# Moving the first V weights' low halves from GpSimd to VectorE, with newly searched order tables, in a one-core kernel of a hybrid attention and RWKV-7 layer

## The chip, the cores and the metric

The kernel runs on one core of one Trainium2 chip. The metric is the device time of one execution in microseconds (us); lower is better. The engines are TensorE (PE in the profile, with PEld for its weight loads), VectorE (DVE), ScalarE (ACT), GpSimd (POOL) and SyncE (SP), which issues nearly all DMA transfers here. Each engine carries out its own queue of instructions in the order in which the program wrote them.

## The reference

One layer of a decoder trunk, with sequence length 512 and width 1024, in float32:

```
ada = c @ w_ada + b_ada                       # 6 x 1024: shift, scale, gate for two blocks
h = rms_norm(x, norm1_w) * (1 + sc1) + sh1
proj = h @ w_in                               # attention q/k/v, RWKV-7 r/k/v and low rank, gates
y_att = attention_mixer(att_in) @ w_att_out   # three groups (window, dilation), combined by softmax
y_rwkv = rwkv7_mixer(rwkv_in, ...) @ w_rwkv_out
x = x + gt1 * ((g_att * y_att + g_rwkv * y_rwkv) @ w_o)
h = rms_norm(x, norm2_w) * (1 + sc2) + sh2
x = x + gt2 * conv_ffn(h, w_up, conv_w, conv_b, w_down)
return rms_norm(x, norm_f_w)
```

The RWKV mixer first mixes each of its inputs with that of the token before: z + (z_prev - z) * mu. That is the "shift" of the kernel.

## The kernel before, in words

**Split products.** Each large product is made of three matmuls. A matrix a is split into a high half, a cast to a shorter format, and a low half, the difference `a - hi`. The product is then hi*hi + hi*lo + lo*hi (`gemm`, and the same by single matmuls in `body`). For weights, ScalarE casts the high half and VectorE subtracts to get the low one (`split_w`, `weights`: `whi` and `wlo`, L1397 and L1400; 128x1024 numbers at a time). For the hidden state h the names are `hhi` and `hlo`.

**Order of the work.** Nothing runs in the order in which it is written up to about 740 us. The functions `start`, `attention` and `rwkv` hand tasks to the class `Plan`: an engine, an estimated time, the function that emits the instructions, the tasks that it depends on, a priority, and the buffers that it takes and gives back. `Plan.run` (from L245) then plays a small simulation of the engines. Whenever an engine is free, it takes the ready task of the lowest priority number for which buffers are free, and emits its instructions. So the queues of all five engines, SP's DMA queue among them, come out of this simulation. Two tables correct it. `RANKS` adds a number to the priority of a kind of task (the key is engine, name, function and base priority). `HOLDS` gives the time for which TensorE must have run large matmuls before it turns to a task with small ones (its names are in `FEW`). From about 740 us on (RWKV's output product, the mixing with `w_o`, and the convolutional feed-forward) the order is that of the code.

**The start (0 to about 58 us).** The program loads x, runs some matmuls without use to warm TensorE up, and makes the shift `sh` and the scale `g1c` of the first adaptive norm in four chunks of 256 columns. For one chunk, eight blocks `araw` of w_ada, 256 KB each, come by DMA through SP's queue; VectorE multiplies and adds them up into `acc` (L708 for the first block, L710 for the others); TensorE sums over the partitions (`ada`); VectorE adds biases (`biased`, L734 to L736). Meanwhile TensorE transposes x (`tr`, `turn`); ScalarE scales (`ht`, L750) and casts (`hhi`, L757), and VectorE makes `hlo` (L754). With each part of h that is done, two products begin: `early` (the first q and k columns: `rows`, L767, high half L774, low half L777) and `v` (the first V columns, 256 of them: `v_load` L781, `v_hi` on ScalarE L787, `v_lo` on GpSimd L790). The V weights come in four loads `wvraw` of 128x2x256 numbers each, with two buffers.

**The middle (58 to about 740 us).** Products (`body`) with names such as `qk`, `v`, `lg`, `r`, `k` run on TensorE, between them the small matmuls of attention and RWKV. Two PSUM buffers ("mm") hold the results of these products. An RWKV product's buffer is given back when `shift` has read it: ScalarE writes a scaled, moved copy to `sh`, then VectorE adds the rest (L1410). Around 310 us, at the end of attention, VectorE scales the heads' outputs `o` by their shares `pw` (L1283, from PSUM), GpSimd adds the groups into `attT` (L1287), and the RWKV part's low-rank input `lg` and first `r` product are under way; `lg` is shifted into `lt` and its low half is made by L1424 (`la`, `lw`). The sums `xy`, `inv` and their like later are the steps of RWKV's chunked inverse.

Of the kernel before, what the change touches and what calls it, by code (L numbers as in the profile page):

```python
# [39 lines left out]
class Task:  # L40
# [19 lines left out]
    ('ACT', 'gate hi', 'hi', 69.0): -15.59,  # L60
    ('ACT', 'gate hi', 'hi', 70.0): -48.82,
    ('ACT', 'gate hi', 'hi', 79.0): 145.29,
    ('ACT', 'pack', '<lambda>', 3.0): 141.26,
    ('ACT', 'pe', '<lambda>', 0.5): -6.53,
    ('ACT', 'qk01', 'out', 1.0): 75.76,
    ('ACT', 'qk02 hi', 'hi', 16.0): 90.45,
    ('ACT', 'qk11 hi', 'hi', 26.0): 171.77,
    ('ACT', 'r0 hi', 'hi', 41.0): -15.37,
    ('ACT', 'shift', '<lambda>', 1.0): -48.66,
    ('ACT', 'v', 'out', 1.0): 223.26,  # L70
    ('ACT', 'v0 hi', 'hi', 42.0): -7.9,
    ('ACT', 'v12 hi', 'hi', 32.0): -40.94,
    ('ACT', 'v4 hi', 'hi', 54.0): 94.86,
    ('ACT', 'v6 hi', 'hi', 60.0): 83.03,
    ('ACT', 'v7 hi', 'hi', 63.0): 247.01,
    ('DMA', '', 'g2_load', 2.0): 45.89,
    ('DMA', 'ada', 'load', 2.0): 0.01,
    ('DMA', 'ada', 'load', 4.0): 0.08,
    ('DMA', 'ada', 'load', 13.0): -168.52,
    ('DMA', 'ada', 'load', 15.0): -44.69,  # L80
    ('DMA', 'ada', 'load', 21.0): 4.66,
    ('DMA', 'ada', 'load', 26.0): -4.53,
    ('DMA', 'ada', 'load', 34.0): 1.61,
    ('DMA', 'ada', 'load', 44.0): 15.07,
    ('DMA', 'ada', 'load', 46.0): 17.01,
    ('DMA', 'gate', 'load', 64.0): 9.03,
    ('DMA', 'gate', 'load', 66.0): -6.21,
    ('DMA', 'gate', 'load', 67.0): -17.61,
    ('DMA', 'gate', 'load', 73.0): 127.85,
    ('DMA', 'gate', 'load', 76.0): 3.06,  # L90
    ('DMA', 'gate', 'load', 79.0): 177.78,
    ('DMA', 'lg', 'load', 38.0): -6.6,
    ('DMA', 'pa', 'load', 81.0): -34.81,
    ('DMA', 'pa', 'load', 84.0): -56.19,
    ('DMA', 'pa', 'load', 85.0): -6.11,
    ('DMA', 'pa', 'load', 86.0): -82.28,
    ('DMA', 'pa', 'load', 87.0): -28.22,
    ('DMA', 'pr', 'load', 88.0): 3.83,
    ('DMA', 'pr', 'load', 89.0): 1.56,
    ('DMA', 'qk11', 'load', 26.0): -1.88,  # L100
    ('DMA', 'qk12', 'load', 18.0): -4.01,
    ('DMA', 'qk12', 'load', 30.0): -4.2,
    ('DMA', 'r0', 'load', 41.0): -3.39,
    ('DMA', 'r4', 'load', 53.0): -23.25,
    ('DMA', 'v rows', 'v_load', 2.5): 0.85,
    ('DMA', 'v rows', 'v_load', 3.5): -0.05,
    ('DMA', 'v rows', 'v_load', 5.5): -0.77,
    ('DMA', 'vec', 'load', 2.0): 0.01,
    ('DMA', 'vec', 'load', 10.0): -33.87,
    ('DVE', '', '<lambda>', 200.0): -147.45,  # L110
    ('DVE', '', '<lambda>', 200.2): -44.67,
    ('DVE', '', '<lambda>', 200.3): 4.02,
    ('DVE', '', '<lambda>', 200.4): -161.3,
    ('DVE', '', '<lambda>', 200.6): -199.61,
    ('DVE', '', '<lambda>', 220.0): -140.0,
    ('DVE', '', 'diagonal', 200.25): -181.98,
    ('DVE', '', 'diagonal', 200.65): -127.76,
    ('DVE', '', 'gated', 150.0): -114.98,
    ('DVE', '', 'k_row', 200.0): -171.17,
    ('DVE', '', 'k_row', 200.2): -185.79,  # L120
    ('DVE', '', 'k_row', 200.6): 0.74,
    ('DVE', '', 'l2_lo', 1.0): -18.87,
    ('DVE', '', 'r_k', 200.2): -200.85,
    ('DVE', '', 'scaled', 200.65): -190.19,
    ('DVE', '', 'var', 150.0): 253.2,
    ('DVE', 'ada', 'step', 1.5): 239.91,
    ('DVE', 'ada', 'step', 46.0): -43.16,
    ('DVE', 'gate lo', 'lo', 68.0): 335.19,
    ('DVE', 'pts', 'turned', 1.02): 8.9,
    ('DVE', 'qk10 lo', 'lo', 6.0): 29.84,  # L130
    ('DVE', 'qk11 lo', 'lo', 13.0): 93.21,
    ('DVE', 'scan', '<lambda>', 200.7): -137.91,
    ('DVE', 'shift', '<lambda>', 1.0): 110.56,
    ('DVE', 'v1 lo', 'lo', 45.0): 21.1,
    ('DVE', 'v12 lo', 'lo', 19.0): 36.25,
    ('DVE', 'vec', '<lambda>', 1.0): -1.64,
    ('PE', 'ada', 'cols', 1.0): 47.99,
    ('PE', 'ada', 'rows', 1.0): 9.01,
    ('PE', 'early', '<lambda>', 10.21): 35.75,
    ('PE', 'early', '<lambda>', 10.5): 18.33,  # L140
    ('PE', 'early', '<lambda>', 10.6): 1.32,
    ('PE', 'gate', '<lambda>', 73.0): -81.73,
    ('PE', 'gate', '<lambda>', 75.0): -73.35,
# [2536 lines left out]
```

## Time and profile before

| | |
|---|---|
| median of 3 runs | 1179.42 us (1178.59 to 1179.48) |
| the profiled execution's own time | 1178.59 us |
| its span in the profile | 1176.9 us |
| share of the span busy | PE 98%, PEld 80%, DVE 63%, ACT 46%, POOL 12% |
| instructions on DVE and POOL | 1245 and 275 |
| moved by DMA | 138.94 MB |

The profile is that of one execution. A row of a timeline gives the start in us from the span's beginning, the duration, engine, line, operation, output and inputs by the program's names with their shapes, how many alike were put together, and in brackets the idle time of the engine before it with what ended it. A row of the stretches gives the busy us of PE, PEld, DVE, ACT and POOL with instruction counts, TensorE's granted clock (1.00 is full speed), the busy share of the DMA engines and their GB/s. A row of the waits gives who waited for whom, the total in us, how often, and the longest. All matmuls go through the helper at L339 and all transposes through L342, so one tells them apart by their outputs' names.

### The profile page before, as it was taken

How to read it: one execution, taken by the hardware profiler on the slowest of the kernel's cores; microseconds unless marked ns; L12 is line 12 of the kernel's file. 1: busy time of each engine (PE TensorE's matmuls, PEld its weight loads, DVE VectorE, ACT ScalarE, POOL GpSimd, SP SyncE). 2: the span in 40 equal slices, each digit the busy share in tenths (PEclk: the TensorE clock that was granted, in tenths of full speed). 3: DMA queues.
4: the chain of work that ended last, by engine and by line, in shares of the span. 5: the costliest groups of instructions: out<-in, count | busy, mean ns of one | idle time of the engine just before them, and what ended most of it. 6: DMA issues, size and time to landing. Idle time of an engine off the chain costs nothing.

```text
span 1176.9 us, 19259 instructions
## 1 busy us (share of the span) xinstructions
PE 1158.0 (98%) x7552; PEld 939.6 (80%) x7552; DVE 744.4 (63%) x1245; ACT 541.8 (46%) x1012; POOL 137.5 (12%) x275
## 2 busy tenths in 40 slices
PE   8999999999999999999999999999999999999997
PEld 8888888798677777778877777888888888888886
DVE  6688857423778988656897665844666565552236
ACT  5466524424466374565635653534444444432123
POOL 6110000000300022340101441023000000000001
PEclk9999999999999999999999999999999999999999
DMA  9756767120332332322241526631333333333231
GB/s 326 230 159 187 215 187 220 52 68 19 96 94 73 104 106 75 104 85 87 80 115 59 191 69 197 206 116 37 90 90 101 96 92 106 90 114 101 90 126 72
DMA packets 168330, 138.94 MB, mean 118 GB/s; under 512 B 8785, under 2 KB 150315, under 8 KB 168239
## 3 DMA queue, kind: packets, MB, share of 16 engines
q1 hardware_dynamic: 168095, 137.39, 38.4%
q8 instruction: 59, 0.97, 0.4%
q10 hardware_dynamic: 144, 0.33, 0.1%
q14 instruction: 32, 0.26, 0.1%
HBM read 127.39 MB, written 10.30 MB: 117 GB/s over the span
## 4 chain that ended last, share of the span: by engine, by line
PE 87%; DVE 7%; DMA 3%; ACT 1%; issue 1%; SPq 1%; POOL 0%; POOLq 0%; DVEq 0%; ACTq 0%
PE u L339 23%; PE o L339 13%; PE qk L339 9%; PE v L339 8%; PE pg L339 8%; PE pr L339 4%; PE k L339 3%; PE r L339 3%; PE pa L339 2%; PE pt L342 2%; PE xy L339 2%; PE sc L339 2%; DMA araw<-in_w_ada_dram 1%; PE xo L339 1%; PE po L339 1%
## 5 line engine op out<-in xcount | busy, mean ns | idle before, releaser
L385 DVE TENSOR_TENSOR wlo<-raw,whi 128x1024 fp32r<-128x1024 f32 x65 | 79.6, 1224 | 133.8 <-ACT whi L384 133.8
L339 PE MATMUL u<-h2hi,whi 128*128 128x512 f32 (+2 forms) x368 | 140.6, 382 | 0.0
L339 PE MATMUL u<-h2lo,whi 128*128 128x512 f32 (+2 forms) x368 | 140.6, 382 | 0.0
L339 PE MATMUL u<-h2hi,wlo 128*128 128x512 f32 (+2 forms) x368 | 140.5, 382 | 0.0
L1397 ACT CAST whi<-raw 128x1024 fp32r<-128x1024 f32 (+1 forms) x73 | 72.5, 993 | 122.0 <-PE qk L339 51.1
L384 ACT CAST whi<-raw 128x1024 fp32r<-128x1024 f32 x65 | 68.5, 1054 | 91.6 <-PE o L339 53.7
L1400 DVE TENSOR_TENSOR wlo<-raw,whi 128x1024 fp32r<-128x1024 f32 (+1 forms) x73 | 86.5, 1184 | 31.2 <-ACT whi L1397 31.0
L339 PEld LDWEIGHTS u<-h2lo,whi 128*128 128x128 f32 x368 | 69.1, 188 | 13.4 <-POOL h2lo L596 0.2
L339 PEld LDWEIGHTS u<-h2hi,whi 128*128 128x128 f32 x368 | 69.1, 188 | 13.2
L339 PEld LDWEIGHTS u<-h2hi,wlo 128*128 128x128 f32 x368 | 69.1, 188 | 12.9
L2495 DVE SCALAR_TENSOR_TENSOR u<-u,cols,u 128x511 f32<-128x511 f32 x88 | 65.7, 746 | 4.3 <-ACT u L2493 2.7
L339 PE MATMUL qk<-hhi,whi 128*128 128x512 f32 x160 | 63.4, 396 | 0.0
L339 PE MATMUL qk<-hhi,wlo 128*128 128x512 f32 x160 | 63.1, 394 | 0.0
L339 PE MATMUL qk<-hlo,whi 128*128 128x512 f32 x160 | 62.8, 393 | 0.0
L339 PE MATMUL o<-whi,fhi 128*128 128x512 f32 x144 | 56.1, 390 | 0.3 <-DVE u L2495 0.3
L339 PE MATMUL o<-wlo,fhi 128*128 128x512 f32 x144 | 56.0, 389 | 0.0
L339 PE MATMUL o<-whi,flo 128*128 128x512 f32 x144 | 56.0, 389 | 0.0
L339 PE MATMUL pg<-hhi,whi 128*128 128x512 f32 x128 | 52.2, 408 | 0.4 <-DVE v L1410 0.4
L339 PE MATMUL pg<-hhi,wlo 128*128 128x512 f32 x128 | 51.8, 405 | 0.0
L339 PE MATMUL pg<-hlo,whi 128*128 128x512 f32 x128 | 51.6, 403 | 0.0
L538 DVE SCALAR_TENSOR_TENSOR acc<-araw,cols,acc 128x1024 f32<-128x1024 f32 x28 | 35.8, 1279 | 19.3 <-DMA araw<-in_w_ada_dram 19.1
L1043 DVE CUSTOM_DVE_ANT_0 sm<-sc,m 128x256 f32<-128x256 f32 (+1 forms) x64 | 23.8, 402 | 32.0 <-PE sc L339 30.8
(462 smaller groups left out, 2778.7 us busy)
## 6 DMA issues: line engine op xcount, KB each, us to landing
raw<-in_w_in_dram SPq DMA_DIRECT2D x62, 512.0 KB
raw<-in_w_up_dram SPq DMA_DIRECT2D x44, 512.0 KB
araw<-in_w_ada_dram SPq DMA_DIRECT2D x32, 512.0 KB
raw<-in_w_down_dram SPq DMA_DIRECT2D x22, 512.0 KB
araw<-in_w_ada_dram SPq DMA_DIRECT2D x32, 256.0 KB
wvraw<-in_w_in_dram SPq DMA_DIRECT2D x20, 256.0 KB
raw<-in_w_rwkv_out_dram SPq DMA_DIRECT2D x8, 512.0 KB
raw<-in_w_o_dram SPq DMA_DIRECT2D x8, 512.0 KB
```

The costliest lines, as they stand in the source:

```text
L339: return self.nc.tensor.matmul(out, lhsT, rhs, start=start, stop=stop)
L342: self.nc.tensor.matmul(out, in_, self.ident[: in_.shape[0], : in_.shape[0]], is_transpose=True, start=start, stop=stop,)
L384: self.nc.scalar.copy(hl[0], raw)
L385: (lo_eng or self.nc.vector).tensor_tensor(hl[1], raw, hl[0], op=ALU.subtract)
L538: nc.vector.scalar_tensor_tensor(d["acc"], raw, ck, d["acc"], op0=ALU.mult, op1=ALU.add)
L1043: nc.vector.tensor_tensor_reduce(d["sm", h][:, :wd], d["sc"][h][:, :wd], m[:, 256 - wd : 256] if gi == 0 else m[:, :wd], 1.0, 3.0e38, op0= ...
L1397: nc.scalar.copy(d["w"][0], d["raw"])
L1400: nc.vector.tensor_tensor(d["w"][1], d["raw"], d["w"][0], op=ALU.subtract)
L2495: nc.vector.scalar_tensor_tensor(u[:, d:], pu[:, : S - d], ch(c), u[:, d:], op0=ALU.mult, op1=ALU.add)
```

## The change

There are two edits. In `start`, the function `v_lo` subtracts on VectorE in place of GpSimd, and its task is given to VectorE's queue with an estimate of 0.7 us in place of 1.6. And the tables `RANKS` and `HOLDS` are replaced by others: nearly all entries differ, and so the simulation gives all queues another order up to about 740 us. The program is 7 lines shorter, so a line of the kernel after has a number lower by 7 (L1410 is L1403 after).

```diff
 RANKS = {
-    ('DMA', 'v rows', 'v_load', 2.5): 0.85,
-    ('DVE', 'shift', '<lambda>', 1.0): 110.56,
...
             def v_lo(c=c, w=w):
-                nc.gpsimd.tensor_tensor(vd["w"][1][:, 2 * c : 2 * c + 2], w["v"], vd["w"][0][:, 2 * c : 2 * c + 2],
+                nc.vector.tensor_tensor(vd["w"][1][:, 2 * c : 2 * c + 2], w["v"], vd["w"][0][:, 2 * c : 2 * c + 2],
                                         op=ALU.subtract)
...
-            vt = pool(1.6, v_lo, [t], 2.1, give=("wvraw",), name="v lo")
+            vt = dve(0.7, v_lo, [t], 2.1, give=("wvraw",), name="v lo")
```

GpSimd has 261 instructions in its queue in place of 265, VectorE 1238 in place of 1234, TensorE 5007 rows in both, of the same matmuls. Runs of matmuls of 256 or more columns are broken by smaller ones 199 times in place of 202. Three places follow, of the two programs apart.

SyncE's DMA queue at the start, between the w_ada blocks of chunk 2 and those of chunk 3 (`araw`); `wvraw` are V weights, `raw` with x2 the q and k weights of `early`, `raw` of 128x8x128 a weight load of `body`. Before:

```order
L781 DMA wvraw_364<-in_w_in_dram 128x2x256
L781 DMA wvraw_371<-in_w_in_dram 128x2x256
L767 DMA raw_378<-in_w_in_dram 128x2x256 x2
L369 DMA raw_394<-in_w_in_dram 128x8x128
L700 DMA araw_409<-in_w_ada_dram 128x2x256
```

The same place after:

```order
L774 DMA wvraw_364<-in_w_in_dram 128x2x256
L760 DMA raw_371<-in_w_in_dram 128x2x256 x2
L362 DMA raw_384<-in_w_in_dram 128x8x128
L362 DMA raw_401<-in_w_in_dram 128x8x128
L774 DMA wvraw_415<-in_w_in_dram 128x2x256
L693 DMA araw_423<-in_w_ada_dram 128x2x256
```

A second `body` load has moved ahead of chunk 3's blocks, and the second V load behind the q, k and `body` loads.

VectorE's queue at the end of chunk 3 and the beginning of chunk 4 (`acc` are the sums of w_ada blocks, `wv` the V weights' halves, `sh` and `g1c` the biases' results). Before:

```order
L710 SCALAR_TENSOR_TENSOR acc_453<-araw_471,cols,acc_453 128x512
L710 SCALAR_TENSOR_TENSOR acc_453<-araw_481,cols,acc_453 128x512
L708 TENSOR_SCALAR acc_549<-araw_518,cols 128x512
L710 SCALAR_TENSOR_TENSOR acc_549<-araw_527,cols,acc_549 128x512
L734 TENSOR_TENSOR sh_111<-ada_551,cols 128x2
L735 TENSOR_TENSOR g1c<-ada_551,cols 128x2
L736 SCALAR_TENSOR_TENSOR g1c<-g1c,cols 128x2
L710 SCALAR_TENSOR_TENSOR acc_549<-araw_533,cols,acc_549 128x512
```

The same place after:

```order
L703 SCALAR_TENSOR_TENSOR acc_469<-araw_488,cols,acc_469 128x512
L703 SCALAR_TENSOR_TENSOR acc_469<-araw_495,cols,acc_469 128x512
L783 TENSOR_TENSOR wv_392<-wvraw_415,wv_391 128x512
L701 TENSOR_SCALAR acc_548<-araw_521,cols 128x512
L727 TENSOR_TENSOR sh_111<-ada_536,cols 128x2
L728 TENSOR_TENSOR g1c<-ada_536,cols 128x2
L729 SCALAR_TENSOR_TENSOR g1c<-g1c,cols 128x2
L770 TENSOR_TENSOR wlo_542<-raw_501,whi_541 128x1024
L703 SCALAR_TENSOR_TENSOR acc_548<-araw_527,cols,acc_548 128x512
```

One of the four moved subtractions stands behind chunk 3's last block, and the biases stand one block earlier in chunk 4.

VectorE's queue around 310 us of the profile before (`o` scaled by `pw`, then the low halves and the shifts; `lt<-lg` is the shift of the low-rank input). Before:

```order
L1283 TENSOR_TENSOR o_117<-o_117,pw_3049 128x512
L1283 TENSOR_TENSOR o_117<-o_117,pw_3054 128x512
L1283 TENSOR_TENSOR o_117<-o_117,pw_3059 128x512
L1283 TENSOR_TENSOR o_117<-o_117,pw_3069 128x512
L1400 TENSOR_TENSOR wlo_3066<-raw_2984,whi_3065 128x1024
L1424 TENSOR_TENSOR la<-lt_2993,la 64x512
L1410 SCALAR_TENSOR_TENSOR lt_3095<-lg_3001,mu_2_121,sh 32x512
L1400 TENSOR_TENSOR wlo_3098<-raw_2853,whi_3097 128x1024
L1410 SCALAR_TENSOR_TENSOR k_3119<-r_2979,mu_120,sh 128x512
```

The same place after:

```order
L1263 TENSOR_TENSOR share<-pe_3038,share 8x512
L1403 SCALAR_TENSOR_TENSOR lt_3058<-lg_2989,mu_2_121,sh 32x512
L1276 TENSOR_TENSOR o_117<-o_117,pw_3061 128x512
L1393 TENSOR_TENSOR wlo_3055<-raw_2977,whi_3054 128x1024
L1276 TENSOR_TENSOR o_117<-o_117,pw_3063 128x512
L1276 TENSOR_TENSOR o_117<-o_117,pw_3072 128x512
L1276 TENSOR_TENSOR o_117<-o_117,pw_3087 128x512
L1428 TENSOR_SCALAR lt_3058<-lt_3058 32x512
L1393 TENSOR_TENSOR wlo_3100<-raw_1901,whi_3099 128x1024
L1403 SCALAR_TENSOR_TENSOR k_3122<-k_2961,mu_120,sh 128x512
```

The shift of `lg` has moved ahead of the four scalings and of the low half `wlo`, and the split `la` no longer stands here but about thirty rows earlier.

More of the change, by code (lines that the diff above doesn't have):

```diff
@@ L60 @@
[L60 to L95, printed above, removed]
@@ L108 @@
[L108 to L131, printed above, removed]
@@ new lines @@
+    ('ACT', 'pts', 'turned', 1.0): 211.5,
+    ('ACT', 'qk01', 'out', 1.0): 29.09,
+    ('ACT', 'qk01 hi', 'hi', 12.0): 49.1,
+    ('ACT', 'qk12 hi', 'hi', 17.0): -28.85,
+    ('ACT', 'r4 hi', 'hi', 53.0): -52.65,
+    ('ACT', 'v0 hi', 'hi', 42.0): 167.12,
+    ('ACT', 'v12 hi', 'hi', 19.0): 218.37,
+    ('ACT', 'v4 hi', 'hi', 54.0): 202.52,
+    ('DMA', 'ada', 'load', 2.0): -35.02,
+    ('DMA', 'ada', 'load', 3.0): -14.22,
+    ('DMA', 'ada', 'load', 19.0): 1.45,
+    ('DMA', 'ada', 'load', 25.0): -1.05,
@@ new lines @@
+    ('DMA', 'ada', 'load', 35.0): -1.19,
+    ('DMA', 'gate', 'load', 64.0): 1.55,
+    ('DMA', 'gate', 'load', 67.0): -2.21,
+    ('DMA', 'gate', 'load', 68.0): 6.69,
+    ('DMA', 'gate', 'load', 69.0): -6.31,
+    ('DMA', 'gate', 'load', 73.0): 116.59,
+    ('DMA', 'gate', 'load', 79.0): 160.33,
+    ('DMA', 'lg', 'load', 38.0): -12.76,
+    ('DMA', 'lg', 'load', 39.0): 1.1,
+    ('DMA', 'pa', 'load', 81.0): 4.99,
+    ('DMA', 'qk00', 'load', 4.0): -4.27,
+    ('DMA', 'qk00', 'load', 5.0): -4.9,
@@ new lines @@
+    ('DMA', 'qk01', 'load', 11.0): -5.78,
+    ('DMA', 'qk01', 'load', 25.0): -5.77,
+    ('DMA', 'qk02', 'load', 29.0): 5.91,
+    ('DMA', 'qk11', 'load', 27.0): 6.78,
+    ('DMA', 'r7', 'load', 62.0): -1.38,
+    ('DMA', 'rows', 'rows', 2.5): -19.57,
+    ('DMA', 'rows', 'rows', 3.5): -7.21,
+    ('DMA', 'v rows', 'v_load', 2.5): -6.43,
+    ('DMA', 'v1', 'load', 45.0): -21.04,
+    ('DMA', 'v2', 'load', 48.0): 13.86,
+    ('DMA', 'v4', 'load', 54.0): -22.65,
+    ('DMA', 'vec', 'load', 2.0): -50.64,
@@ new lines @@
+    ('DMA', 'x', 'load', 2.0): -53.8,
+    ('DVE', '', '<lambda>', 0.0): -46.28,
+    ('DVE', '', '<lambda>', 1.0): -46.33,
+    ('DVE', '', '<lambda>', 200.0): -5.42,
+    ('DVE', '', '<lambda>', 200.1): -222.9,
+    ('DVE', '', '<lambda>', 200.2): -264.85,
+    ('DVE', '', '<lambda>', 200.3): 114.14,
+    ('DVE', '', 'g2_lo', 150.0): -138.65,
+    ('DVE', '', 'k_row', 200.2): -147.35,
+    ('DVE', '', 'l2_lo', 1.0): 200.47,
+    ('DVE', '', 'r_k', 200.6): -190.77,
+    ('DVE', '', 'recip', 200.25): -179.41,
```

211 lines of the change are left out of this document (109 added, 102 removed).

## The prediction

> **What bounds the kernel now.** I read the page first, then the table of stretches, then the chain's waits on TensorE, then the timelines of TensorE, VectorE, GpSimd and ScalarE around the waits. From the page:
>
> ```profile
> span 1176.9 us, 19259 instructions
> PE 1158.0 (98%) x7552; PEld 939.6 (80%) x7552; DVE 744.4 (63%) x1245; ACT 541.8 (46%) x1012; POOL 137.5 (12%) x275
> ```
>
> TensorE is busy for 1158.0 of 1176.9 us. The change leaves its matmuls as they are and only reorders them, so the whole prize is 18.9 us of idle time plus what a lowered clock adds. GpSimd, with 137.5 us, is not a bound anywhere by its own time. The stretches (busy us of PE, PEld, DVE, ACT and POOL with their instruction counts, then the granted clock, the DMA share and GB/s) tell where to look:
>
> ```profile
> 20.00:40.00 20.00, 17.65 (x106) 15.09 (x106) 18.58 (x25) 7.82 (x11) 9.17 (x10) 1.00 1.10 342
> 300.00:320.00 20.00, 17.43 (x75) 11.87 (x74) 17.56 (x27) 8.65 (x16) 6.63 (x5) 0.92 0.30 93
> 360.00:420.00 60.00, 58.62 (x417) 46.79 (x418) 53.60 (x97) 29.21 (x45) 2.59 (x7) 1.00 0.31 87
> 580.00:620.00 40.00, 39.67 (x313) 31.88 (x313) 37.63 (x74) 15.87 (x23) 1.22 (x5) 1.00 0.37 103
> 23.35:26.76 3.41, 1.96 (x9) 1.30 (x7) 3.30 (x4) 1.70 (x3) 2.07 (x2) 1.00 1.15 319
> 37.00:40.42 3.42, 2.21 (x16) 1.67 (x14) 2.97 (x3) 0.62 (x1) 3.01 (x2) 1.00 1.09 348
> 40.42:43.83 3.41, 2.98 (x12) 2.86 (x13) 3.31 (x9) 2.69 (x4) 0.00 (x0) 0.50 1.15 322
> 313.48:316.90 3.42, 1.02 (x5) 0.52 (x3) 3.36 (x3) 1.04 (x1) 2.74 (x2) 1.00 0.47 145
> 316.90:320.31 3.41, 3.24 (x8) 2.56 (x9) 2.80 (x4) 1.77 (x3) 0.79 (x2) 0.50 0.57 179
> ```
>
> In the two 20-us stretches TensorE is idle for 2.35 and 2.57 us while VectorE is nearly full. Inside each lies a piece of 3.41 us at clock 0.50. Each such piece follows one in which TensorE was little busy (2.21 and 1.02 of 3.42 us). Work that took 2.98 us at half clock would take 1.49 at full clock, so the pieces cost 1.5 and 1.6 us. TensorE's waits, in us in total, times and longest:
>
> ```profile
> PE v L339 <- DVE lt L1410: 2.6, 1, 2.6
> PE ada L339 <- DVE acc L710: 1.8, 2, 1.6
> PE tr L342 <- DVE g1c L735: 1.4, 1, 1.4
> PE k L339 <- DVE k L1410: 0.9, 1, 0.9
> PE pg L339 <- DVE v L1410: 0.4, 1, 0.4
> ```
>
> The three waits above 1 us are all for VectorE, and all lie in those two stretches. These are where the change can give, and the terms of the sum.
>
> **The move from GpSimd to VectorE (20 to 58 us).** Timelines (start, us, engine, line, operation, idle time before and what ended it) of GpSimd, VectorE, ScalarE and TensorE:
>
> ```profile
> 24.69 3.24 POOL L790 TENSOR_TENSOR wv<-wvraw,wv 128x512 fp32r<-128x512 f32 x2 [1.77 <-ACT wv L787]
> 37.00 3.02 POOL L790 TENSOR_TENSOR wv<-wvraw,wv 128x512 fp32r<-128x512 f32 x2 [9.06 <-ACT wv L787]
> 25.17 1.64 DVE L710 SCALAR_TENSOR_TENSOR acc<-araw,cols,acc 128x512 f32<-128x512 f32 x1
> 29.66 1.22 DVE L1400 TENSOR_TENSOR wlo<-raw,whi 128x1024 fp32r<-128x1024 f32 x1
> 30.84 0.69 DVE L754 TENSOR_TENSOR hlo<-ht,hhi 128x512 fp32r<-128x512 f32 x1
> 31.45 0.74 DVE L710 SCALAR_TENSOR_TENSOR acc<-araw,cols,acc 128x512 f32<-128x512 f32 x1
> 38.91 1.65 DVE L710 SCALAR_TENSOR_TENSOR acc<-araw,cols,acc 128x512 f32<-128x512 f32 x1
> 40.56 0.14 DVE L735 TENSOR_TENSOR g1c<-ada,cols 128x2 f32<-128x2 f32 x1
> 28.12 1.05 ACT L1397 CAST whi<-raw 128x1024 fp32r<-128x1024 f32 x1 [0.77 <-DMA raw<-in_w_in_dram]
> araw<-in_w_ada_dram SPq DMA_DIRECT2D x32, 256.0 KB
> 26.86 1.05 PE L339 MATMUL ada<-few,acc 128*128 128x1 f32 x8 [1.55 <-DVE acc L710]
> 37.62 1.02 PE L339 MATMUL ada<-few,acc 128*128 128x1 f32 x8 [0.26 <-DVE acc L710]
> 40.85 1.09 PE L342 MATMUL tr<-ident,xt 128*128 128x128 f32 x4 [1.38 <-DVE g1c L735]
> ```
>
> The four L790 subtractions take about 1.6 us each on GpSimd (3.24 / 2, 3.02 / 2). While one runs, a VectorE instruction with two SBUF inputs is stretched: the same accumulation L710 takes 1.64 and 1.65 us beside GpSimd and 0.74 without it, a loss of 0.9 us each time. So the change removes at least two such losses, 1.8 us of VectorE. It adds four subtractions of 128x512 to VectorE. The trace does not show them there; the equal shape L754 takes 0.69, which I take, 4 x 0.69 = 2.8 us. The lower bound is 0.62 (half of the 1.22 that L1400 takes for twice the columns), the upper 1.6 (if something else on GpSimd runs beside it). VectorE's total thus hardly changes (+1.0 us); what changes is when each step ends.
>
> Walk of chunk 2 of adaLN: the accumulation that starts at 25.17 ends at 25.9 in place of 26.8, so TensorE's *ada* sums start at 26.0 and 0.85 of the 1.55 us wait goes. Then the new subtraction (to 26.6) and wlo (to 27.9) stand ahead of the biases and g1c (to 28.2 with three at 0.14); TensorE has its v product meanwhile, so this costs nothing unless v's own weights come late. A second body weight load is now queued on SP ahead of chunk 3's first araw. ScalarE's cast shows that a body weight landed at about 28.1; three transfers of 256 KB at 342 GB/s take 2.3 us, so that araw lands near 30.4, and VectorE waits there for about 0.9 us. Eight accumulations then end chunk 3 at 37.5, where it ended before; the 0.26 us wait becomes about 0.85. Chunk 4's first step and the biases follow one subtraction and are not stretched: g1c ends at about 39.5 instead of 40.7. TensorE has its sums and 12 v matmuls until 39.9, so the 1.38 us wait at the transpose goes. In all 1.8 + 1.4 = 3.2 us of waits become 1.8: **1.4 us gained**. If the piece from 37.00 is then busy enough, the half clock after it goes too: **1.5 us**. Term: -2.9; bounds +0.5 (the waits at chunk 3 become longer and the half clock stays) to -4.2 (all the waits but 0.5 go).
>
> **The order at 300 to 320 us.** VectorE, GpSimd and TensorE:
>
> ```profile
> 311.96 2.35 DVE L1400 TENSOR_TENSOR wlo<-raw,whi 128x1024 fp32r<-128x1024 f32 x1
> 314.34 1.90 DVE L1424 TENSOR_TENSOR la<-lt,la 64x512 fp32r<-64x512 f32 x1
> 316.28 0.74 DVE L1410 SCALAR_TENSOR_TENSOR lt<-lg,mu,sh 32x512 f32<-32x512 f32 x1
> 310.12 3.10 POOL L1287 TENSOR_TENSOR attT<-o,o 128x512 f32<-128x512 f32 x2 [11.77 <-DVE o L1283]
> 314.16 3.47 POOL L1287 TENSOR_TENSOR attT<-o,o 128x512 f32<-128x512 f32 x2 [0.94 <-DMA att_d<-attT]
> 317.07 0.79 PE L339 MATMUL v<-hhi,whi 128*128 128x512 f32 x1 [2.57 <-DVE lt L1410]
> ```
>
> TensorE has no PSUM buffer for v until the shift L1410 has read lg. The shift itself takes 0.74 us; it stands behind a wlo of 2.35 (1.22 alone) and an la of 1.90, both stretched by GpSimd's attT. In the new order the shift stands right behind *share*, ahead of four o scalings and of wlo; la was done far earlier. So 2.57 us of wait and 1.6 us of half clock go. The new order has three shorter exposures instead: lg's own buffer behind *share* (one 0.7 us instruction), the last o scaling pw_3087 behind wlo (it waits about 0.75 us), and v's next buffer (0.35): 1.8 us. Term: 2.57 + 1.6 - 1.8 = **-2.4**, with bounds 0 (the last scaling and the k shift, now behind a stretched wlo, hold TensorE as long as lt did) and -4.2 (none of the three is exposed).
>
> **The rest of the order.** Counted in the two orders, a run of matmuls of 256 columns or more is broken by small ones 202 times before and 199 after. A break costs about 0.2 us:
>
> ```profile
> 280.47 0.72 PE L339 MATMUL sc<-qk,qk 64*128 64x128 f32 x8
> 281.12 0.50 PE L339 MATMUL lg<-hhi,wlo 128*128 128x512 f32 x1
> 281.45 0.40 PE L339 MATMUL lg<-hhi,whi 128*128 128x512 f32 x1
> ```
>
> After the small sc matmuls 0.33 us pass from the start of the first large one to that of the next. Undisturbed, such a step is half of the 0.43 that it takes at half clock, 0.22 us:
>
> ```profile
> 318.09 0.63 PE L339 MATMUL v<-hhi,wlo 128*128 128x512 f32 x1
> 318.52 0.63 PE L339 MATMUL v<-hhi,whi 128*128 128x512 f32 x1
> ```
>
> So leaving a break costs 0.11 us; I choose the same for entering one, 0.2 in all. Term: 3 x 0.2 = **-0.6**, bounds 0 and -0.6. Everything from about 740 us on stands in the same order and is taken at nothing. Elsewhere (60 to 300, 320 to 740 us) the new tables reorder much, but the largest of TensorE's waits there are the 0.9 and 0.4 us above, so little is to be had and more can be lost: see the rivals.
>
> **Sum.** -2.9 - 2.4 - 0.6 = -5.9 against the profiled execution's 1178.59 us (its span 1176.9 and 1.69 around it): 1172.7. That execution was 0.83 us below the median of the three runs, 1179.42, so the forecast is **1173.5** against the median. A measurement of this kernel tells about 0.2%, 2.4 us, from no change: faster is below 1177.06, slower above 1181.78.
>
> **The rivals.**
>
> A, slower. New stalls like the one at 314 us arise where VectorE is full: it is busy 53.6 of 60 us from 360 and 37.6 of 40 us from 580. Mechanism: a shift that frees a PSUM buffer, queued behind a wlo (1.22 us, 2.35 if GpSimd runs) and steps of the inverse; TensorE then lacks a buffer, and a 3.41-us piece at half clock follows. Each costs 2.57 + 1.6 = 4.2 us. Two of them: 1173.5 + 8.4 = 1181.9, slower; it decides from 8.3 us of new waits and clock. For: the two orders differ most there. Against: before shows only 0.9 and 0.4 us of such waits in the whole remainder, with a VectorE as full.
>
> B, no change. One such stall: 1173.5 + 4.2 = 1177.7.
>
> C, the half-clock pieces stay although the waits go, or move: -5.9 + 3.1 gives 1176.6. For it: the clock seems to be decided on pieces of 3.41 us in which little work ran, and how the waits fall across their borders is chance; the piece from 23.35, with a wait of 1.55 us and 1.96 us busy, did not lower the clock, while 37.00, with 2.21 busy, did. The Trainium skill, "TensorE: Matmul & The Clock Gate", section "Why this matters for your kernels", says that the clock falls when TensorE idles for more than about 3 us between bursts. By that rule the waits of 1.38 and 2.57 us could not have lowered it, and ending them would not raise it, which is this rival; the trace disagrees, since both pieces at 0.50 follow just these waits.
>
> D, more than forecast. The new waits at 310 us do not come (1.8), the first term comes out at its better end (1.3 more), and the waits for k (0.9) and pg (0.4) go too: 1173.5 - 4.4 = 1169.1. For it: each of these waits is for VectorE, and the shift goes ahead of wlo in the one place where I followed it. Against: three separate things must go well.
>
> That the move does nothing can be excluded as far as GpSimd goes, since the four rows stand in VectorE's order; that it changes only when waits come and not their sum is rival B's time.
>
> **How the numbers follow.** Forecast 45%, A 13%, B 17%, C 12%, D 13%. Faster than 1177.06 are the forecast, C and D: 0.70; B is the same: 0.17; A slower: 0.13. The forecast's own bounds, with all terms at their worst, are 1173.5 + 3.4 + 2.4 + 0.6 = 1179.9, and at their best 1173.5 - 1.3 - 1.8 = 1170.4. The range leaves A out and takes in B, C and D with 0.6 us below D, should the breaks be worth twice their price: 1168.5 to 1181.0.
>
> **What would show it.** Right, if the new profile has no L790 subtraction on GpSimd, L703 accumulations at 0.75 us throughout chunks 2 to 4, no wait at the transpose for g1c, no piece at clock 0.50 near 40 or 317 us, and less than 2 us of waits from 300 to 320. Wrong, if *ada* waits longer than 2 us in sum, if v or k wait for a shift behind wlo, or if a stretch between 360 and 720 us shows TensorE idle for 2 us or a clock below 1.00.

## The result and the profile after

The kernel after takes 1172.72 us (median of 6 runs, 1171.28 to 1176.2), before 1179.77 us (6 runs, 1178.59 to 1181.8). The ratio is 0.994, with a 95% interval of 0.9924 to 0.9956: 7.1 us faster, between 5.2 and 9.0. The forecast was 1173.5 us, that is 5.9 us faster. The profiled execution after took 1172.75 us, 5.84 us less than the profiled one of before. From its page:

```profile
span 1171.0 us, 19239 instructions
PE 1155.3 (99%) x7552; PEld 936.3 (80%) x7552; DVE 740.9 (63%) x1249; ACT 544.1 (46%) x1012; POOL 132.3 (11%) x271
```

TensorE's idle time fell from 18.9 to 15.7 us, and its busy time by 2.7 us with the same 7552 matmuls; the two pieces of lowered clock that are gone, 3.1 us by the prediction's estimate, come to about that. The stretches after, with the columns of the prediction:

```profile
20.00:40.00 20.00, 18.56 (x103) 14.87 (x103) 17.76 (x29) 8.87 (x12) 3.53 (x10) 1.00 1.11 337
40.00:60.00 20.00, 20.00 (x132) 18.18 (x131) 13.59 (x22) 10.64 (x15) 0.00 (x0) 1.00 0.61 179
300.00:320.00 20.00, 20.00 (x91) 14.49 (x90) 14.63 (x27) 8.18 (x14) 7.10 (x5) 1.00 0.39 118
```

Both half-clock pieces have gone (1.00 in all three rows), and from 300 to 320 us TensorE has no idle time at all. TensorE's waits after:

```profile
PE ada L332 <- DVE acc L703: 2.0, 3, 0.7
PE qk L332 <- DVE qk L931: 0.6, 1, 0.6
PE vec L335 <- DMA rows<-in_b_ada_dram: 0.5, 1, 0.5
```

The waits for g1c (1.4), for lt (2.6) and for k (0.9) are gone; nothing above 0.7 us is left in one piece beside the start-up wait of 1.4 us that both kernels have. The start, on VectorE and then on TensorE:

```profile
26.61 0.68 DVE L783 TENSOR_TENSOR wv<-wvraw,wv 128x512 fp32r<-128x512 f32 x1
31.12 0.49 DVE L701 TENSOR_SCALAR acc<-araw,cols 128x512 f32<-128x512 f32 x1 [0.89 <-DMA araw<-in_w_ada_dram]
38.19 0.68 DVE L783 TENSOR_TENSOR wv<-wvraw,wv 128x512 fp32r<-128x512 f32 x1
39.84 0.15 DVE L728 TENSOR_TENSOR g1c<-ada,cols 128x2 f32<-128x2 f32 x1
26.74 1.05 PE L332 MATMUL ada<-few,acc 128*128 128x1 f32 x8 [0.70 <-DVE acc L703]
38.42 1.02 PE L332 MATMUL ada<-few,acc 128*128 128x1 f32 x8 [0.55 <-DVE acc L703]
```

The moved subtraction takes 0.68 us, the 1.55 us wait is 0.70, and no transpose waits. Near 310 us, on VectorE and GpSimd:

```profile
307.99 0.74 DVE L1403 SCALAR_TENSOR_TENSOR lt<-lg,mu,sh 32x512 f32<-32x512 f32 x1
309.58 1.22 DVE L1393 TENSOR_TENSOR wlo<-raw,whi 128x1024 fp32r<-128x1024 f32 x1
309.81 2.44 POOL L1280 TENSOR_TENSOR attT<-o,o 128x512 f32<-128x512 f32 x1 [12.93 <-DVE o L1276]
```

The shift is done at 308.7 us. TensorE needs its buffer for r when k's 24 matmuls end at about 312.9, so 4.2 us are to spare. The next buffer is closer: v takes that of k at 316.09 us, 0.2 us after k's shift has ended. The wlo started 0.23 us ahead of the addition on GpSimd and takes its 1.22 us, although the two then ran side by side for 1.0 us; here the addition is the longer one, 2.44 us where the three after it take 1.6 each.

**Where the time went, by stage.** To compare two orders of the same matmuls, I gave each kind of matmul its usual step to the next start and asked when each kernel had started the same total of such steps. Against before, the profile after stood at +0.73 us at 24.6 us, at -2.10 at 62 us, at -1.3 at 295 us, at -6.1 at 342 us and at -5.83 at the end. So the start gave 2.83 us, the place near 310 us about 4.8, and the rest took 1.1 back (0.8 before 295 us). The +0.73 at 24.6 us has no cause in the change: it is there at 20 us already, the first 26 loads stand in the same order in both, and the wait for vec above, absent before, shows one of them landing later. The new order's other profiles stood at +0.56, +0.57 and 0.0 there, and of the runs below e3 and e7, with the old order of loads, at +1.15 and +1.19. Between quiet points of different orders such a difference is good to some 0.5 us. From one execution to the next it moves by more: with the start of before unchanged, e5 and e6 lost nothing between 24.6 and 62 us, but e10 1.5 and e3 2.2 us.

### The profile page after: what moved, and what is told of

The parts are those of the page before. It is cut to its first block, busy times and chain, and to the rows that moved or that the text cites. A ratio compares the mean times of both kernels' runs of the same rounds, so it can differ in the third digit from the quotient of the medians.

```text
span 1171.0 us, 19239 instructions
## 1 busy us (share of the span) xinstructions
PE 1155.3 (99%) x7552; PEld 936.3 (80%) x7552; DVE 740.9 (63%) x1249; ACT 544.1 (46%) x1012; POOL 132.3 (11%) x271
## 4 chain that ended last, share of the span: by engine, by line
PE 86%; DVE 7%; DMA 3%; issue 1%; ACT 1%; SPq 1%; POOL 0%; POOLq 0%; DVEq 0%; ACTq 0%
PE u L332 23%; PE o L332 13%; PE v L332 8%; PE qk L332 8%; PE pg L332 7%; PE pr L332 4%; PE k L332 4%; PE r L332 3%; PE pa L332 3%; DMA araw<-in_w_ada_dram 2%; PE pt L335 2%; PE xy L332 2%; PE sc L332 1%; PE xo L332 1%; PE po L332 1%
## 5 line engine op out<-in xcount | busy, mean ns | idle before, releaser
L2240 ACT CAST fhi<-u 128x512 fp32r<-128x512 f32 x22 | 13.7, 621 | 60.9 <-DVE u L2499 60.9
```

Source lines behind the costliest of these rows:

```text
L2240: self.nc.scalar.copy(hi, src)
```

## The experiments

In all edits of an order below, the planner first writes its tasks into a list in the order that it found, the list is changed in the named places, and then the instructions are emitted from it:

```diff
-                t.fn()
+                seq.append(t)
...
+        for t in seq:
+            t.fn()
```

The medians and ratios of each run stand against the kernel before, timed on the same chip. There were three chips, with medians of before of 1179.80 us (e1 to e4), 1181.25 (e5 to e8) and 1180.70 (e9 to e12), so runs of different groups are compared by their ratios:

| run | median, us | ratio to before (95%) | against before at 62, 295, 342 us and at the end, us, one profile |
|---|---|---|---|
| e1_new_order_gpsimd | 1173.34 | 0.9938 (0.9916 to 0.9959) | -0.6, -0.8, -5.6, -5.2 |
| e2_old_order_vector | 1178.33 | 0.9984 (0.9970 to 0.9997) | +0.1, +0.1, +0.4, +2.3 |
| e3_old_order_shift_early | 1180.49 | 0.9998 (0.9980 to 1.0015) | +3.4, +3.5, +3.5, +3.2 |
| e4_both | 1179.30 | 0.9990 (0.9975 to 1.0004) | -1.8, -1.6, -1.5, +0.7 |
| e5_both_shifts | 1179.31 | 0.9988 (0.9972 to 1.0003) | +0.2, +0.3, -2.3, -0.6 |
| e6_no_att_sum | 1177.42 | 0.9969 (0.9956 to 0.9981) | +0.1, +0.4, -3.2, -0.5 |
| e7_start_by_hand | 1177.15 | 0.9966 (0.9955 to 0.9976) | -1.0, -1.1, -0.9, -1.1 |
| e8_both_places | 1174.86 | 0.9951 (0.9935 to 0.9967) | -1.8, -1.7, -4.3, -3.5 |
| e9_three_places | 1181.42 | 1.0000 (0.9982 to 1.0018) | -2.0, -2.1, -4.7, +4.8 |
| e10_spread_only | 1182.00 | 1.0028 (1.0007 to 1.0048) | +2.0, +1.9, +0.8, +1.4 |
| e11_new_order_load_late | 1171.61 | 0.9928 (0.9914 to 0.9942) | -2.6, -2.6, -7.4, -6.6 |
| e12_after_again | 1172.53 | 0.9938 (0.9922 to 0.9953) | -2.4, -2.6, -7.4, -6.8 |

**e1: the new order with the subtractions on GpSimd.**

```diff
-                nc.vector.tensor_tensor(vd["w"][1][:, 2 * c : 2 * c + 2], w["v"], ...
+                nc.gpsimd.tensor_tensor(vd["w"][1][:, 2 * c : 2 * c + 2], w["v"], ...
```

> The kernel after, every queue in its new order, but the four subtractions of the V weights' low halves issued to GpSimd again (the planner still counts them as VectorE's 0.7 us). Theory 1, the move itself carries the gain of the start: beside each of the first two subtractions one accumulation of w_ada is stretched from 0.75 to about 1.65 us, TensorE's ada waits grow by 0.9 and 0.7 us, and a piece at half clock may come back (1.5 us): 1.6 to 3.1 us slower than the kernel after, 1174.3 to 1175.8. Theory 2, the gain of the start comes from the new order of loads and biases alone: the stretching is paid back by 4 x 0.69 us that VectorE no longer spends, and the time stays within 0.5 us of the kernel after, 1172.7.

VectorE, TensorE and two stretches:

```profile
21.85 5.63 DVE L705 SCALAR_TENSOR_TENSOR acc<-araw,cols,acc 128x512 f32<-128x512 f32 x6
31.25 1.77 DVE L749 TENSOR_TENSOR hlo<-ht,hhi 128x512 fp32r<-128x512 f32 x1
27.54 1.05 PE L334 MATMUL ada<-few,acc 128*128 128x1 f32 x8 [1.67 <-DVE acc L705]
26.12:29.53 3.41, 1.99 (x17) 1.99 (x18) 3.33 (x7) 2.23 (x3) 0.03 (x1) 1.00 1.14 325
29.53:32.94 3.41, 3.41 (x18) 3.41 (x18) 2.75 (x3) 1.47 (x3) 1.36 (x1) 0.50 1.10 349
```

The six accumulations of chunk 2 take 5.63 us (4.71 after), hlo 1.77 instead of 0.68, ada waits 1.67 instead of 0.70, and a half-clock piece follows. In the trace the start gains 1.2 us where the kernel after gains 2.83: the move is worth 1.6 us there, the lower end of theory 1. The median of 1173.34 us is below theory 1's range and 0.6 us above the 1172.72 of the kernel after, the ratios are the same (0.9938 and 0.994), and at the end of the two traces 0.6 us are left of the 1.6. So the time of the whole program doesn't decide between the theories; the rows do, for this execution.

**e2: the old order with the subtractions on VectorE.** The opposite edit, in the kernel before.

> The kernel before, every queue in its old order, but the four subtractions issued to VectorE at the same place of the program. Theory 1 (the move carries the gain): no accumulation above 0.8 us, the 1.55 us wait of ada falls to 0.7 or less, the 1.38 us wait at the transpose and the half clock behind it go: 2.5 to 3 us faster than before, about 1177. Theory 2 (the place counts): in the old order two of the four stand ahead of the last accumulations of chunk 2 and two ahead of the biases of chunk 4, where they cost as much as the stretching did; ada starts about 0.25 us earlier, the transpose about 0.3 us earlier, the half clock stays: 0.3 to 0.6 us faster, 1179.3.

On VectorE and TensorE:

```profile
24.71 0.69 DVE L792 TENSOR_TENSOR wv<-wvraw,wv 128x512 fp32r<-128x512 f32 x1 [0.19 <-ACT wv L789]
26.91 1.05 PE L341 MATMUL ada<-few,acc 128*128 128x1 f32 x8 [1.46 <-DVE acc L712]
40.74 1.05 PE L344 MATMUL tr<-ident,xt 128*128 128x128 f32 x4 [1.52 <-DVE g1c L737]
```

Nothing is stretched any more, and still ada waits 1.46 us and the transpose 1.52: the subtraction stands ahead of the last two accumulations and pushes them back by what the stretching cost. This is theory 2: at 62 us this execution stands where before stood. It is not the only outcome: e4, below, has the same start, and there the half-clock piece came at 28.28 us, the transpose waited for nothing, and 1.65 us were gained between 24.6 and 62 us. e2's median is 0.16% lower (0.03 to 0.3%).

**e3 and e4: the shift of lg alone.** e3 is the kernel before with that one VectorE instruction moved; e4 has e2's edit too.

```diff
+        p = [i for i, t in enumerate(seq) if getattr(t, "rows", 0) == 32]
+        if p:
+            seq.insert(p[0] + 1, seq.pop(p[1]))
```

> The kernel before with one VectorE instruction moved: the shift of the low-rank input lg near 316 us goes ahead of one wlo and one la, everything else in its old order. Theory 1 (that shift held TensorE, and the idle time lowered the clock): the shift ends near 312.7 us, before TensorE needs the buffer at 314.35, so the 2.57 us wait and the half-clock piece of 1.6 us go: 4.2 us faster, about 1175.6. Theory 2 (another wait takes its place, the wlo and la pushed back or the next buffer): at least 1.5 us of new waits within 10 us, and 0 to 2.5 us faster. Theory 3 (the clock falls by itself at that time): 2.6 us faster and a piece at 0.50 stays.

> The kernel before with both edits: the four subtractions on VectorE and the shift of lg moved, the rest in the old order. If the two places are independent, the gains add: by theory 1 of both 6.7 to 7.2 us (1172.6 to 1173.1, all that the change brings); with the subtractions worth only 0.3 to 0.6 us, 4.5 to 4.8 us (about 1175.1). The rival is that a gain of the start shifts the free-running pieces by which the clock is set, and a half-clock piece appears elsewhere: less than 3 us.

VectorE and TensorE in e4:

```profile
310.52 0.74 DVE L1415 SCALAR_TENSOR_TENSOR lt<-lg,mu,sh 32x512 f32<-32x512 f32 x1
311.19 1.53 DVE L1405 TENSOR_TENSOR wlo<-raw,whi 128x1024 fp32r<-128x1024 f32 x1
312.75 1.95 DVE L1431 TENSOR_TENSOR la<-lt,la 64x512 fp32r<-64x512 f32 x1
314.74 2.45 DVE L1405 TENSOR_TENSOR wlo<-raw,whi 128x1024 fp32r<-128x1024 f32 x1
317.11 0.74 DVE L1415 SCALAR_TENSOR_TENSOR k<-r,mu,sh 128x512 f32<-128x512 f32 x1
317.90 0.50 PE L344 MATMUL k<-hhi,whi 128*128 128x512 f32 x1 [2.51 <-DVE k L1415]
```

Theory 2, in its clearest form: lt is in time, and the next shift, behind the same stretched wlo, la and a second wlo, holds TensorE for 2.51 us in place of 2.57, with a half-clock piece behind it as before. e3 shows the same 2.51 us at 323. Neither edit gained anything near 310 us.

**e5: both shifts early.** The same, and the next shift ahead of the second wlo as well.

> The kernel before with two VectorE instructions moved: the shift of lg ahead of one wlo and one la (as in the run before that), and the next shift, of r, ahead of the second wlo. Theory 1 (TensorE is held by whichever shift stands behind the stretched instructions; with both early nothing holds it): no wait above 0.5 us and no half clock between 300 and 325 us, 3.7 to 4.2 us faster than before, about 1175.8. Theory 2 (VectorE simply has too much to do there, so the delay moves on to a third place): a wait of 1.5 us or more on wlo or the next shift before 330 us, and less than 2 us faster.

```profile
319.13 0.50 PE L346 MATMUL k<-hhi,wlo 128*128 128x512 f32 x1 [0.99 <-DVE wlo L1407]
```

2.5 us are gained between 295 and 342 us in the trace, and no half clock is left there. A third wait remains, 0.99 us for the wlo that was pushed back. This lies between the two theories: with both shifts early most of the stall goes, and 0.99 of the 2.57 us come back in a third place. Whether VectorE's load alone makes that wait isn't shown, since this wlo too took 1.80 us beside GpSimd. The whole program doesn't show the gain: its ratio of 0.9988 has an interval from 0.9972 to 1.0003, and the 3.7 to 4.2 us of theory 1 lie outside it.

**e6: no addition on GpSimd.**

```diff
-                nc.gpsimd.tensor_tensor(d["t"], o[0][:, i, :], o[1][:, i, :].rearrange("p (r j) -> p j r", r=4), op=ALU.add)
+                nc.gpsimd.memset(d["t"], 0.0)
```

> The kernel before in its old order, but the four additions of the attention groups on GpSimd near 310 us are replaced by filling attT with zeros (the sum of the two groups is left out), so that GpSimd reads nothing there. Theory 1 (the stretching by GpSimd makes the shift late): wlo takes 1.22 in place of 2.35 and la 0.69 in place of 1.90, the shift of lg ends at 314.7, the wait falls from 2.57 to 0.6 or less and the half clock goes: 3.5 to 4 us faster, about 1176. Theory 2 (the order of the instructions alone decides): the wait stays above 1.5 us, 1 us faster or less, about 1179.

```profile
312.40 1.22 DVE L1402 TENSOR_TENSOR wlo<-raw,whi 128x1024 fp32r<-128x1024 f32 x1
313.65 0.69 DVE L1426 TENSOR_TENSOR la<-lt,la 64x512 fp32r<-64x512 f32 x1
315.17 0.50 PE L341 MATMUL v<-hhi,whi 128*128 128x512 f32 x1 [0.22 <-DVE lt L1412]
```

In the old order, without GpSimd's reads, wlo and la take 1.22 and 0.69 us (2.35 and 1.90 before), the wait is 0.22 us and the half clock is gone: 3.6 us in the trace, 3.7 us in the median (ratio 0.9969). Theory 1 holds: in the old order the stall needs the stretching. There are two ways out: take GpSimd's reads away, or let the shifts go ahead of what is stretched. The change took the second, and in its order the wlo beside the first addition wasn't stretched either (1.22 us above).

**e7 and e8: the two places by hand.** In e7 the subtractions are on VectorE and three things stand where the new order has them; e8 adds e5's edit.

```diff
+        f = lambda t: t.fn.__qualname__.split(".")[-1]
+        p = [i for i, t in enumerate(seq) if f(t) == "biased"]
+        if p:
+            b = p[2]
+            k = [i for i, t in enumerate(seq) if i < b and t.eng == "DVE" and f(t) == "step"][-1]
+            seq.insert(k, seq.pop(b))
+            v = [t for t in seq if f(t) == "v_lo"]
+            last = [t for t in seq if t.eng == "PE" and f(t) == "cols"][1]
+            g = [t for t in seq if f(t) == "biased"][1]
+            for t, a in ((v[0], seq.index(last)), (v[1], seq.index(g))):
+                seq.remove(t)
+                seq.insert(a, t)
```

> The kernel before with the four subtractions on VectorE, three things moved by hand as the new order has them, and the old order of loads: the first subtraction behind the last accumulation of chunk 2, the second behind chunk 2's biases, and chunk 3's biases ahead of the second accumulation of chunk 4. Theory 1 (where these few VectorE instructions stand carries the gain of the start): ada's wait falls from 1.55 to 0.7, the wait of 1.38 at the transpose to below 0.3, no half clock before 60 us: 2.5 to 3 us faster, about 1177. Theory 2 (the new order of the loads is needed): the wait at the transpose goes but chunk 3's sums come later by as much, or a half-clock piece stays: 1 us or less, 1179.

> The kernel before with the hand-made start and with both shifts near 315 us moved: some eight instructions in all, the rest in the old order. If these two places are all that the new tables bring: 6 to 7 us faster, 1172.6 to 1173.6, as the kernel after. If the rest of the new order matters too (fewer breaks, other small waits): 1175 or more. If the pieces at half clock only move: one shows elsewhere and 1.5 us are missing.

TensorE at the start of e7:

```profile
27.23 1.05 PE L353 MATMUL ada<-few,acc 128*128 128x1 f32 x8 [0.73 <-DVE acc L724]
38.56 1.02 PE L353 MATMUL ada<-few,acc 128*128 128x1 f32 x8 [0.55 <-DVE acc L724]
44.20 0.39 PE L353 MATMUL v<-wv,hlo 128*128 128x256 f32 x1 [0.69 <-DVE hlo L768]
```

These are the two waits of the kernel after, nearly to the hundredth (0.70 and 0.55), with the old order of loads; the transpose doesn't wait, there is no half clock, and a new wait of 0.69 us for hlo comes. The start gains 2.2 us in the trace, the median falls by 0.34% (0.24 to 0.45%), about 4 us: theory 1, with a median that fell by more than the 2.5 to 3 us expected. e8 comes to 1174.86 us, between its two expectations and next to the second (1175 or more), and shows no half-clock piece before 1170 us. Two of its waits that the kernel after doesn't have, beside that for hlo:

```profile
PE pe L358 <- issue: 1.3, 1, 1.3
PE k L358 <- DVE wlo L1419: 1.0, 1, 1.0
```

So some eight moved instructions bring about 0.5 of the 0.6%. The intervals overlap (0.9935 to 0.9967, and 0.9924 to 0.9956), so it isn't shown that the rest of the new order matters; if it does, the trace offers three places, the wait for hlo, the third wait of e5 and a wait for issue that no step of mine had in it.

**e9 and e10: the wait for issue.** The old order's profiles of before and e2 to e8 all have it between 640 and 670 us, 0.4 to 1.4 us, within a run of small matmuls (in e8 there is no large one from 648.6 to 657.7 us), and four of them (e2, e4, e5, e6) a half-clock piece behind it. Of the new order's four profiles only e12 has one, of 0.4 us. In the new order the planner had put large matmuls of the gate product between some of the groups of small ones. In e9 (on e8) and e10 (on before) I did the same by hand with the last eight of them:

```diff
+        g = [i for i, t in enumerate(seq) if t.eng == "PE" and t.name == "gate"]
...
+            units, read = [seq[i] for i in g[-8:]], last.users[0]
+            pes = [t for t in seq[g[-1]:] if t.eng == "PE" and t.name == "pe" and t.us == 0.45][:6]
+            for t in units + [read]:
+                seq.remove(t)
+            for q, m in zip(pes, (1, 1, 1, 1, 2, 2)):
+                at = seq.index(q) + 1
+                seq[at:at], units = units[:m], units[m:]
```

> The kernel before with both places by hand and a third: near 650 us TensorE ran some nine microseconds of small matmuls alone (from 648.6 to 657.7 in the run before this one) and waited in them for its own issue, 1.26 us there and 0.4 to 1.4 us in all profiles of the old order. Here the last eight large matmuls of the gate product (and the copy that reads it) are moved between the groups of small ones. Theory 1 (TensorE used up its instructions faster than they were fetched; large matmuls between the small ones give the fetch time): no wait for issue there, 1.2 us faster than both places alone, about 1173.5. Theory 2 (the wait comes from something else, such as the number of small matmuls as such or the transfers of that moment): the wait stays, and the added breaks cost 6 x 0.2 us: 1175 to 1176.

> The kernel before with the third place alone: the last eight large matmuls of the gate product moved between the small ones near 655 us, all else old. If the fetch of instructions is the cause: no wait for issue, 0.4 to 1.4 us and, where a half-clock piece followed the wait, 1.7 us more: 1 to 2.5 us faster than before in the median. If not: within 1 us of before.

A wait of e9 between 640 and 670 us, and four of its stretches:

```profile
PE u L369 <- ACT uv L2123: 1.1, 1, 1.1
644.79:648.20 3.41, 2.10 (x67) 1.56 (x67) 3.33 (x8) 2.85 (x8) 1.82 (x3) 1.00 1.03 390
648.20:651.60 3.40, 3.40 (x51) 2.23 (x50) 2.94 (x6) 1.26 (x4) 3.02 (x4) 0.50 0.44 127
651.61:655.03 3.42, 3.42 (x80) 2.18 (x77) 0.00 (x0) 0.89 (x3) 0.82 (x2) 0.50 0.84 282
665.27:668.68 3.41, 3.41 (x52) 2.47 (x52) 0.80 (x3) 2.20 (x5) 0.79 (x3) 0.50 0.24 67
```

The wait for issue is gone from both, and neither is faster: e9 is level with before, where e8 without this edit was 0.49% faster, and e10 is 0.28% slower. Without the large matmuls in their old place, the step u of the inverse comes to its turn before ScalarE has copied uv, and waits 1.1 us (e10: 1.0). In e9's profile this gave a stretch with 2.10 us busy, and the clock stayed at half for six pieces, 20.5 us, in which TensorE was busy all the time, by count mostly with small matmuls. That execution lost 9.5 us after 600 us. Four of e9's twelve executions took 1175.5 to 1176.7 us at a mean granted clock of 0.998, the other eight, this one among them, 1180.0 to 1183.5 us at 0.989 to 0.994. e10's profile, of 1179.97 us, tells nothing of the five of its twelve that took 1187.5 to 1189.3 us.

These two runs alone don't show that spreading large matmuls ended the wait for issue, since the wait for uv stands just ahead of the small groups and gives the same time. What the wait is for can be read from the traces. Instructions come on the queue that the page calls q8, 16 KB at a time. All thirteen waits for issue between 640 and 670 us (twelve in the eight profiles of the old order, one in e12) end 1.2 to 1.5 us behind the landing of such a transfer, and in the old order always in front of the same matmul, the 4797th of the program or the 4670th. In e8 a transfer landed at 654.88 us:

```profile
656.24 0.36 PE L358 MATMUL pe<-lt,lr 32*32 32x16 f32 x20 [1.26 <-issue]
```

In e10 the 4797th came 2.4 us behind the landing, and didn't wait. This is what theory 1 says, a wait for fetched instructions; that q8 serves TensorE is read from this timing, and nothing here took such a transfer away.

**e11 and e12: one load later, and the kernel after again.** e11 is the kernel after with the second body load, ahead of chunk 3's blocks, moved behind them.

```diff
+        ada = [t for t in seq if t.eng == "DMA" and f(t) == "load" and t.name == "ada" and "start" in t.marks]
...
+            seq.remove(body)
+            seq.insert(seq.index(ada[23]) + 1, body)
```

> The kernel after with one load moved: the second weight load of body, which the new order put ahead of chunk 3's w_ada blocks and which is first used after 48 us, goes behind them. If chunk 3 is bound by its loads: VectorE's wait of 0.89 us for the first block and 0.24 us later go, the sums end about 1 us earlier, TensorE's 0.55 us wait goes: 0.5 us faster than the kernel after in the trace of the start, hardly to be told in the medians (1172 to 1172.7). If VectorE's own work binds it: no change in the wait of ada.

> The kernel after unchanged, timed beside the three others: 1172.7 as before, with a profile to tell what varies from run to run. By my reading the 0.75 us by which its first profile ran behind before at 24 us is a late landing of x and not the change, so this profile should stand within 0.3 us of before at the same work there, or vary either way; no wait for issue near 650 us; no half-clock piece before 1160 us.

VectorE and TensorE in e11:

```profile
38.90 0.49 DVE L709 TENSOR_SCALAR acc<-araw,cols 128x512 f32<-128x512 f32 x1 [1.72 <-DMA araw<-in_w_ada_dram]
39.67 0.63 PE L343 MATMUL tr<-ident,xt 128*128 128x128 f32 x4 [0.39 <-DVE g1c L736]
```

The wait for chunk 3's first block goes and TensorE's wait for chunk 3's sums falls from 0.55 to 0.36 us; but chunk 4's first block is waited for 1.72 us, 0.49 in the kernel after: the load has moved, not vanished, and the transpose waits 0.39 us again. At the start e11 gains 2.6 us in the trace, e12 2.9. Its median of 1171.61 us is the lowest, 0.9 us below e12's 1172.53, and five of e12's six executions took longer than all six of e11's, timed beside them. But the trace doesn't show that gain at the place, so e11 is probably a little faster than the kernel after, for a reason that stays open. e12 came as the kernel after had (1172.53 and 1172.72 us), with no half-clock piece before 1165 us; it stood at +0.57 us at 24.6 us, and it has a wait for issue of 0.40 us where none was expected.

## Why the prediction was right, step by step

**The start, -2.9: right in size and mechanism.** Measured from the late beginning of that execution (0.73 us), TensorE's sums of chunk 2 start at 26.0 us as walked, chunk 3's first block lands at 30.4, VectorE waits 0.89 us for it (0.9 walked), g1c ends at 39.3 (39.5), the 1.38 us wait and the half clock go: 2.83 us. The waits of this stretch fell from 3.2 to 1.25 us, further than the walk's 1.8, and with 1.5 us for the clock that makes 3.4; so the size agrees within what the comparison tells, and not to 0.1 us. The sign of being wrong that *ada* waits longer than 2 us was nearly met: 1.98 us, of which 0.73 lie at 16.86 us, ahead of the changed instructions.

The other runs sharpen the reason. Against before, between 24.6 and 62 us, the old places with GpSimd gave 0.0 (e5, e6), 1.5 and 2.2 us of loss (e10, e3); the old places with VectorE 0.0 (e2) and a gain of 1.65 (e4); GpSimd in the new order a gain of 1.2 (e1); VectorE in the places moved by hand 2.1 to 2.3 (e7, e8, e9), and in the new order 2.6 to 2.9 (after, e11, e12). All eight executions without both parts have one or two half-clock pieces before 60 us, none of the six with both has any. So both parts are needed: taking GpSimd off alone gave 0.0 and 1.65 us in its two executions, as the half-clock piece fell, and the steady gain comes when the first two subtractions also stand behind chunk 2's accumulations and the biases go ahead of chunk 4's second. The prediction had this in its walk but gave the losses of 0.9 us first.

**Near 310 us, -2.4: the right wait, mis-sized by 2.4.** Measured: about -4.8 at the quiet points, 0.6 beyond the term's own bound of -4.2, which is about what the comparison can be off by, and no idle time at all from 300 to 320 us. The term that failed is "the new order has three shorter exposures instead ... 1.8 us". It measured 0: those instructions come about where I had them, but k already had its buffer and the shift came 4.2 us before the next product (r, from 312.91 us) needed lg's. The shift of k came 0.2 us before v (from 316.09 us) needed k's, so this one was close. I counted waits of VectorE's instructions and did not follow the two buffers to the matmul that needs each. e3 and e4 show that naming lt as the cause was too narrow too: with lt moved alone the stall is passed on whole.

**The breaks, -0.6: not found.** Outside the two places the kernel after lost 1.1 us and e12 0.4 (-0.2 before 295 us, +0.6 after 342 us). Three breaks of 202 can't be told from such differences.

**The sum.** That the forecast came within 0.8 us is in part luck, since its errors cancel: -2.83 and -4.8 with +0.73 and +1.1 make the -5.83 of the trace, next to the forecast -5.9. The ratio's 7.1 us is more than the profiles differ, because the profile of before was that of its fastest execution, 1.2 us below the median of the six. Its wait for issue, which may be part of that, was 0.4 us without a half-clock piece, where five of the eight profiles of the old order named above have 1.3 us or more, and four a piece.

**The rivals.** A and B did not come: after 320 us no wait of the kernel after is above 0.4 us. Their mechanism is real, though: e4 is just that, a shift behind stretched wlo. C did not come: both pieces at 0.50 went with their waits. That a piece hangs on more than its wait, as C has it, is so all the same: in e10 TensorE waited 2.56 us for the same shift of lg, and no piece followed. The rule of the Trainium skill, "TensorE: Matmul & The Clock Gate", section "Why this matters for your kernels", that was weighed there (gaps above about 3 us) is contradicted by these runs: single waits of 1.1 (e9), 1.67 (e1) and 2.51 us (e4) were followed by such pieces too, and none was above 3 us. D came in part, at 310 us.

## What to carry to other kernels

When a wait ends on a late instruction, list what else stands behind the same slow instructions on that engine: moving only the one that the profile names passes the stall on to the next. Follow each new wait to the buffer and the work that needs it before it is counted. And moving work off a slow engine pays by where it then stands: the same four subtractions gave 0 and 1.65 us in the two executions with the old places, and 2.1 us or more in all six with the new.

## What the runs showed of the hardware

Up to the last piece, which ends with the kernel, the pieces of lowered clock are 3.41 us or a multiple (6.83 in e10, 20.48 in e9), at distances that are multiples of it (40.42 and 316.90 us before: 81 pieces). Each followed a stretch of 3.41 us on that grid in which TensorE was busy 0.9 to 2.9 us, but 23.35 to 26.76 us before, with 1.96 busy, was followed by none. Nor was either of the two stretches over which the 2.56 us wait of e10 fell:

```profile
314.61:318.03 3.42, 1.82 (x9) 1.16 (x7) 3.39 (x2) 1.04 (x1) 2.50 (x3) 1.00 0.43 151
318.03:321.44 3.41, 2.45 (x11) 2.04 (x12) 3.38 (x5) 1.20 (x2) 1.59 (x2) 1.00 0.72 222
```

So busy time alone doesn't set it, and what does stays open. The Trainium skill, "TensorE: Matmul & The Clock Gate", section "What's actually happening", has such a free-running window of 3413 ns, and the traces agree. It also says that a busy window of that length brings full speed back; e9 disagrees, with TensorE busy 3.41 of 3.41 us at 0.50 in stretch after stretch of mostly small matmuls. Small matmuls alone didn't lower the clock either: e8 ran nothing else from 648.64 to 655.47 us, at 1.00.

In these profiles, which of VectorE and GpSimd loses time beside the other goes by which started first. Up to 330 us, in all fourteen, each VectorE instruction that was lengthened beside a two-input GpSimd operation of over 1 us started while that operation ran. Those that had started before it kept their time, and beside an accumulation or a wlo it was then the GpSimd operation that took longer. In the kernel before, the accumulation at 24.38 us, 0.31 us ahead of GpSimd, takes 0.75 us, and the next, at 25.17, 1.64; in the kernel after, the wlo at 309.58 us keeps 1.22 and the addition takes 2.44 us.

An instruction of VectorE with a single input was lengthened beside GpSimd as well. On VectorE in the kernel after, ahead of GpSimd's addition and beside it:

```profile
301.35 0.43 DVE L1428 TENSOR_SCALAR lt<-lt 128x512 f32<-128x512 f32 x1
312.80 1.26 DVE L1428 TENSOR_SCALAR lt<-lt 32x512 f32<-32x512 f32 x1
```

The same line takes 0.43 and 1.26 us (0.41 for the smaller shape in the kernel before, at 319.30 us, when GpSimd ran nothing). The shift, which reads PSUM, kept its 0.74 us beside GpSimd: in the kernel before it ran from 316.28 us, wholly inside an addition of GpSimd.
